# Another order of the 52 tiles of the first input projection

## The chip, the cores and the metric

The kernel runs on one core of a Trainium2 chip. The metric is the device time of one execution in microseconds; of the kernel before there are three runs, with a median of 2320.35 us (2316.67 to 2329.12). A profile of one more execution shows what each engine did: TensorE (PE, with its weight loads as PEld), VectorE (DVE), ScalarE (ACT), GpSimd (POOL) and SyncE (SP), which issues the DMAs.

## The reference

One inference step of a two-layer decoder for a prompt of 512 tokens and 8 x 4 sample tokens (544 columns in all), float32, width 2048. The first ("even") layer:

```python
h = x @ w_in                       # 2048 -> 6784 = 53 blocks of 128
h_sh, gate_a, q_b, k_b, v_b, gate_b, q_m, gate_m = _split(h, (...))
prev = concatenate([shift0[:, None], h_sh[:, :-1]])
y_a, s_new = rwkv7_mix(h_sh + (prev - h_sh) * mu, ...)   # 12 heads x 64, a recurrence
y_b = combine(...)                 # dilated windows: 3 groups x 4 heads x 64
y_m = memory_attention(q_m, mkv)   # 4 heads x 128, 256 memory tokens
u = concatenate([y_a * silu(gate_a), y_b * silu(gate_b), y_m * silu(gate_m)])
x = layer_norm(ALPHA * x + u @ w_out, ln_g, ln_b)
```

The second ("odd") layer has the same frame with a retention branch. Both groups of tokens share all weights; the sample tokens also read cached keys, values and states. Returned are the two outputs and all new states.

## The kernel before

Everything is laid out with features in partitions and the 544 tokens in columns. A *tile* is one block of 128 output features of a projection. Its 16 blocks of weights are loaded by SP (two halves, four buffers in all), split into a high part by ACT and a low part by DVE, and multiplied with the split activations in three matmuls per block (`three`, line 469), for two halves of 272 columns: 96 matmuls a tile. Behind each half, ACT (for gates also DVE) evacuates it (`done`).

The tiles run in one list (`Main.run`, line 481): eight tiles for the memory keys and values, then the 53 tiles of the first input projection, the output projection, and the second layer. The first projection begins with the tile of the two small `lora` inputs (`r18`, place 0 here); the other 52 follow in the order of the string `ORDER0` (line 2206), each letter taking the next tile of its kind. I call the letters places 1 to 52. The kinds:

- `r`: the 18 blocks of the shifted input of the recurrence, in six triples; with the third of a triple the *pair* of heads is complete and its work is started (pairs 0 to 5; `hsh_done`, line 793). An `r` tile asks for two work buffers and keeps one.
- `q` and `m`: the four queries of the memory attention, and its four gates.
- `b`: the 18 blocks of the dilated windows, for two head pairs: three queries, three keys, three values each. The ninth starts the first head pair's softmax (`b_prompt`), the twelfth the sample keys (`b_keys`), the eighteenth the second softmax and the sample values.
- `a` and `c`: the six gates of the recurrence (one for each pair) and the two of the windows.

All else that a layer does is *side work*: generators (`spawn`, line 302) that a planner at build time steps in between the matmuls of the tiles, two matmul triples apart (`pump`, line 327), by priority. It runs on a model of the engines' clocks; what comes out is a fixed order of instructions for each engine. A pair's work is a long chain: `rwkv_pre` (preparation, priority 1, begins with a load of `lora` weights), `rwkv_solve` (a triangular solve in 31 steps on DVE, instructions of 102 partitions), `rwkv_chain` (eight chunks of small dependent matmuls), `rwkv_sample` (loads `rwkv_s`, started when half of the chain is done) and `rwkv_norm`, which stores the result to `yad`; a gate tile reads it back, multiplies, and the product is split for the output projection.

Side work and tiles share 41 work buffers of 128 x 576 floats (tag `P`). A pair reserves 13 of them before its `lora` load (`open`, line 107), a softmax 8, the sample keys 7, the sample values 9. A reservation begins only when that many are free beyond what is promised to others. A tile that needs a buffer where all free ones are promised makes the planner step side work alone until one comes free (`drive`, line 339):

```python
def page(self, dt=F32, cols=PAGE, own=None, wait=True):
    if wait and own is None and self.avail('P') <= self.held():
        self.drive(lambda: self.avail('P') > self.held())
```

The output projection takes its 12 blocks of gated results in the order in which their gates stand in `ORDER0` (`out_order`, line 2211), and its first tile drives side work until the blocks are there (`Gated.mov`, line 1877).

Of the kernel before, what the change touches and what calls it, by code (L numbers as in the profile page):

```python
# [2202 lines left out]


MEM0 = (0, 1, 2, 3, 4, 5, 6, 7)
ORDER0 = 'rrqrbbqrqqrrrrrmbrmbbbrbrmbrbmarrbabrarraabbbbbbbcca'
ORDER1 = '0000000011111111222222223333333344444444qqqq55555555mmmm'
SPILL1 = (0, 1, 2, 3, 4, 5, 6, 7, 8, 9)

# [1 line left out]
def out_order():  # L2211

    ks0, ks = [], {'a': list(range(6)), 'c': [6, 7], 'm': list(range(8, 12))}
    for ch in ORDER0:
        if ch in ks:
            ks0.append(ks[ch].pop(0))
    ks1, left = [], {c: ORDER1.count(c) for c in ORDER1}
    for ch in ORDER1:
        left[ch] -= 1
        if ch == 'm':  # L2220
            ks1.append(15 - left[ch])
        elif ch != 'q' and left[ch] < 2:
            ks1.append(2 * int(ch) + 1 - left[ch])
    return ks0, ks1


def body(nc, tc, A, npages=41, stop=None):
    from contextlib import ExitStack
    with ExitStack() as es:
# [92 lines left out]
        ks0, ks1 = out_order()  # L2322
        for ch in ORDER0:
            order.append(kinds[ch].pop(0))
# [256 lines left out]
```

## Time and profile before

| | us |
|---|---|
| median of three runs | 2320.35 |
| the profiled execution | 2316.73 |
| its span, first to last instruction | 2314.9 |
| TensorE busy | 2206.6 (95%) |
| VectorE, ScalarE, GpSimd busy | 1294.8, 980.8, 296.1 |
| mean granted clock of TensorE | 0.977 |

Of TensorE's time, the matmuls of the tiles take most; the first input projection lies between about 58 and 1034 us. Busy times are unions over an engine's instructions. A granted clock of 1.00 is 2.4 GHz, and 0.5 is the lower level of 1.2 GHz; a mean between them says what part of a stretch was at which level.

### The profile page before, as it was taken

What the parts mean: (1) busy time and instruction counts of PE and PEld (TensorE: products, weight loads), DVE (VectorE), ACT (ScalarE), POOL (GpSimd) and SP (SyncE); (2) the same over time, 40 slices, a digit from 0 to 9 for tenths busy, and PEclk for the clock granted to TensorE, in tenths of its full rate; (3) what the DMA queues carried; (4) which work ended last, traced back from release to release, by engine and by line L of the source; (5) the groups of instructions that cost most, each with busy time, mean ns of one, the idle gap of its engine ahead of it and who ended that gap; (6) DMA issues with size and microseconds to landing.
All of it is one profiled execution on the core that took longest, in us unless ns stands there. A gap on an engine that the chain in (4) does not pass through costs nothing. (4 is left out here: it accounts for less than half of the span.)

```text
span 2314.9 us, 46280 instructions
## 1 busy us (share of the span) xinstructions
PE 2206.6 (95%) x18633; PEld 2118.7 (92%) x18633; DVE 1294.8 (56%) x2718; ACT 980.8 (42%) x2286; POOL 296.1 (13%) x445
## 2 busy tenths in 40 slices
PE   8999999889998999998989999999999999999996
PEld 8999898778998989887979999999999999999996
DVE  6367468637656766355788444444444433347686
ACT  6344453356244444343577323232323243235464
POOL 0000000000000000002665000000000000003474
PEclk9999999989999999998999999999999999999998
DMA  9222532312221424528757443424343424445662
GB/s 328 99 72 78 202 99 85 103 52 98 76 71 52 122 82 130 189 72 275 211 164 249 161 131 102 134 99 137 97 137 97 141 84 171 144 167 183 214 205 100
DMA packets 149714, 313.46 MB, mean 135 GB/s; under 512 B 39376, under 2 KB 48536, under 8 KB 149500
## 3 DMA queue, kind: packets, MB, share of 16 engines
q1 hardware_dynamic: 149500, 310.51, 41.3%
q8 instruction: 146, 2.39, 0.4%
q14 instruction: 68, 0.56, 0.1%
HBM read 271.38 MB, written 39.07 MB: 134 GB/s over the span
## 5 line engine op out<-in xcount | busy, mean ns | idle before, releaser
L194 PE MATMUL m<-xh,wh 128*128 128x272 f32 (+1 forms) x4448 | 1323.5, 298 | 9.4 <-ACT wh L227 3.8
L194 PE MATMUL m<-xh,wl 128*128 128x272 f32 (+1 forms) x4448 | 1289.3, 290 | 8.7 <-DVE wl L235 8.6
L194 PE MATMUL m<-xl,wh 128*128 128x272 f32 (+1 forms) x4448 | 1286.1, 289 | 3.5 <-DVE xl L235 3.5
L194 PEld LDWEIGHTS m<-xh,wh 128*128 128x128 f32 x4448 | 845.0, 190 | 23.6 <-issue 9.5
L194 PEld LDWEIGHTS m<-xh,wl 128*128 128x128 f32 x4448 | 842.6, 189 | 11.8 <-DVE wl L235 11.7
L194 PEld LDWEIGHTS m<-xl,wh 128*128 128x128 f32 x4448 | 845.1, 190 | 6.8 <-DVE xl L235 3.8
L235 DVE TENSOR_TENSOR wl<-wr,wh 128x512 fp32r<-128x512 f32 (+1 forms) x752 | 548.1, 760 | 445.5 <-ACT wh L227 439.6
L227 ACT ACTIVATE wh<-wr 128x512 fp32r<-128x512 f32 (+1 forms) x752 | 419.1, 604 | 248.2 <-PE m L194 230.1
L235 POOL TENSOR_TENSOR P<-P,P 128x272 f32<-128x272 f32 (+1 forms) x242 | 244.7, 1033 | 897.6 <-ACT P L227 733.5
L194 PE MATMUL s<-P,P 128*128 128x128 f32 (+11 forms) x3808 | 331.9, 283 | 27.7 <-ACT P L227 15.6
L194 PEld LDWEIGHTS s<-P,P 128*128 128x128 f32 (+6 forms) x3808 | 256.4, 145 | 73.1 <-ACT P L227 22.0
L227 ACT ACTIVATE P<-m 128x272 f32<-128x272 f32 (+3 forms) x253 | 93.8, 379 | 513.4 <-PE m L194 513.0
L235 DVE TENSOR_TENSOR P<-P,P 128x544 f32<-128x544 f32 (+24 forms) x576 | 279.7, 497 | 54.5 <-ACT P L227 34.8
L227 ACT ACTIVATE P<-s 64x64 f32<-64x64 f32 (+9 forms) x581 | 160.1, 291 | 346.9 <-PE s L194 121.6
L227 ACT ACTIVATE P<-P 64x64 f32<-64x64 f32 (+5 forms) x284 | 124.6, 451 | 125.4 <-POOL P L235 72.7
L240 DVE SCALAR_TENSOR_TENSOR P<-P,m 128x272 f32<-128x272 f32 x116 | 50.4, 435 | 134.2 <-ACT P L227 97.8
L284 POOL MEMSET P<- 128x576 f32 (+6 forms) x104 | 28.9, 291 | 569.3 <-PE s L194 316.0
L194 PE MATMUL m<-P,wh 128*128 128x256 f32 x352 | 68.5, 295 | 8.3 <-ACT wh L227 6.4
L209 PE MATMUL s<-cst,P 128*128 128x128 f32 (+2 forms) x409 | 64.5, 283 | 12.1 <-ACT P L227 8.8
L194 PEld LDWEIGHTS m<-P,wh 128*128 128x128 f32 x352 | 57.7, 201 | 9.3 <-ACT wh L227 6.6
L267 DVE TENSOR_REDUCE P<-P 102x1 f32<-102x2 f32 (+16 forms) x193 | 60.9, 315 | 6.7
L209 PEld LDWEIGHTS s<-cst,P 128*128 128x128 f32 (+2 forms) x409 | 49.3, 142 | 15.0 <-ACT P L227 9.1
(69 smaller groups left out, 926.9 us busy)
## 6 DMA issues: line engine op xcount, KB each, us to landing
wr<-w_in SPq DMA_DIRECT2D x218, 512.0 KB
wr<-w_out SPq DMA_DIRECT2D x64, 512.0 KB
wr<-w_out SPq DMA_DIRECT2D x64, 384.0 KB
wr<-w_mem SPq DMA_DIRECT2D x26, 512.0 KB
P<-ret_s SPq DMA_DIRECT2D x48, 256.0 KB
o_ret_s<-P SPq DMA_DIRECT2D x48, 256.0 KB
P<-dk SPq DMA_DIRECT2D x36, 256.0 KB
P<-dv SPq DMA_DIRECT2D x36, 256.0 KB
```

The source lines that it names most:

```text
L194: self.nc.tensor.matmul(out, lhsT, rhs, start=start, stop=stop, skip_group_check=True)
L209: self.nc.tensor.transpose(out, in_, ident)
L227: self.nc.scalar.activation(out, in_, func, **kw)
L235: e.tensor_tensor(out, a, b, op=op)
L240: self.nc.vector.scalar_tensor_tensor(out, a, s, b, op0=op0, op1=op1)
L267: self.nc.vector.tensor_reduce(out, a, axis=AX.X, op=op)
L284: e.memset(out, v)
```

## The change

One string: the order of the 52 tiles. The tiles themselves, the side work and its priorities and all sizes stay. The order of the blocks in the output projection follows from the string: before it is the four `m`, five `a`, two `c`, the last `a`; after it is the four `m`, four `a`, the first `c`, two `a`, the second `c`.

```diff
 MEM0 = (0, 1, 2, 3, 4, 5, 6, 7)
-ORDER0 = 'rrqrbbqrqqrrrrrmbrmbbbrbrmbrbmarrbabrarraabbbbbbbcca'
+ORDER0 = 'rrrbbqrqqqrrrrrrmbmbbbrbbmbrrrbrmaabrarrbacabbbbbbac'
 ORDER1 = '0000000011111111222222223333333344444444qqqq55555555mmmm'
```

## Rows read from the trace of the kernel before

**Rows 1.** The page: span, and busy us (share of the span) and instructions by engine.

```profile
span 2314.9 us, 46280 instructions
...
PE 2206.6 (95%) x18633; PEld 2118.7 (92%) x18633; DVE 1294.8 (56%) x2718; ACT 980.8 (42%) x2286; POOL 296.1 (13%) x445
...
PEclk9999999989999999998999999999999999999998
```

**Rows 2.** Busy us of engines by stage: PE, PEld, DVE, ACT, POOL, granted clock, DMA share, GB/s.

```profile
106.80:311.30 204.50, 201.64 (x1699) 190.06 (x1698) 114.14 (x292) 95.26 (x255) 11.09 (x44) 0.99 0.35 115
311.30:445.50 134.20, 125.60 (x1045) 121.40 (x1044) 103.64 (x283) 53.35 (x119) 5.34 (x30) 0.99 0.33 98
445.50:594.80 149.30, 126.38 (x944) 116.95 (x946) 89.24 (x208) 74.06 (x209) 4.24 (x21) 0.89 0.23 72
775.50:937.10 161.60, 150.13 (x1366) 143.00 (x1369) 102.55 (x258) 71.94 (x195) 6.98 (x26) 0.97 0.38 119
1034.00:1068.60 34.60, 24.17 (x454) 19.96 (x453) 12.48 (x45) 12.85 (x26) 1.26 (x4) 0.70 0.91 323
1260.00:2100.00 840.00, 840.00 (x6823) 819.82 (x6823) 353.43 (x688) 280.63 (x614) 14.77 (x18) 1.00 0.39 132
```

**Rows 3.** Waits of PE, 70 to 1069 us: total us, times, longest.

```profile
PE s L194 <- ACT P L227: 15.6, 15, 2.1
PE s L209 <- ACT P L227: 8.8, 1, 8.8
```

**Rows 4.** Busy us by stage again, for the stretch around place 25.

```profile
445.50:480.00 34.50, 21.03 (x169) 18.58 (x167) 17.74 (x42) 11.42 (x39) 1.11 (x5) 0.65 0.22 56
```

**Rows 5.** Timeline of ACT: evacuations of tiles; start us, us, instruction, idle before.

```profile
106.80 0.40 ACT L227 ACTIVATE P<-m 128x272 f32<-128x272 f32 x1 [1.97 <-PE m L194]
...
123.17 0.37 ACT L227 ACTIVATE P<-m 128x240 f32<-128x240 f32 x1 [1.67 <-PE m L194]
...
445.50 0.40 ACT L227 ACTIVATE P<-m 128x272 f32<-128x272 f32 x1 [1.97 <-PE m L194]
...
474.60 0.40 ACT L227 ACTIVATE P<-m 128x272 f32<-128x272 f32 x1
...
554.59 0.37 ACT L227 ACTIVATE P<-m 128x240 f32<-128x240 f32 x1 [0.63 <-PE m L194]
...
775.52 0.38 ACT L227 ACTIVATE P<-m 128x240 f32<-128x240 f32 x1 [1.98 <-PE m L194]
```

**Rows 6.** Timeline of SP: DMA issues of the pairs, the keys and the softmax.

```profile
120.67 0.42 SPq L288 DMA_DIRECT2D P<-lora  x1
...
293.27 0.38 SPq L288 DMA_DIRECT2D P<-lora  x1
...
316.40 0.33 SPq L288 DMA_DIRECT2D yad<-P  x1
316.82 0.38 SPq L288 DMA_DIRECT2D P<-lora  x1
...
471.01 0.42 SPq L288 DMA_DIRECT2D P<-rwkv_s  x1
...
517.48 0.38 SPq L288 DMA_DIRECT2D P<-lora  x1
...
798.01 0.42 SPq L288 DMA_DIRECT2D yad<-P  x1
798.47 0.43 SPq L288 DMA_DIRECT2D P<-lora  x1
...
914.15 0.43 SPq L288 DMA_DIRECT2D P<-dk  x1
...
959.78 0.38 SPq L288 DMA_DIRECT2D P<-c_bmask  x1
...
1054.46 0.33 SPq L288 DMA_DIRECT2D yad<-P  x1
```

**Rows 7.** Timeline of DVE: the end of pair 2's solve, and what follows.

```profile
459.98 0.52 DVE L267 TENSOR_REDUCE P<-P 102x11 f32<-102x352 f32 x1
460.53 0.28 DVE L240 SCALAR_TENSOR_TENSOR P<-s,P,P 64x64 f32<-64x64 f32 x1
```

**Rows 8.** Timeline of PE: the first matmul of the output projection that waits.

```profile
1062.84 0.60 PE L194 MATMUL m<-xl,wh 128*128 128x272 f32 x1 [3.46 <-DVE xl L235]
```

## The prediction

> **What bounds the kernel now.** I read the profile from the outside in. First the line of busy times and the line of TensorE's clock by slices [rows 1]: TensorE is busy for 95% of the span, so every stall on it counts, and no other engine comes near. Then the busy times by stage [rows 2], to see where the missing 5% sits. From 1260 to 2100 us, in the second layer, TensorE is busy for 840.00 of 840.00 us at a granted clock of 1.00: nothing can be won there. The change lies in the first input projection and what follows on it, and there the stages leave idle 2.9 us of 204.5, 8.6 us of 134.2, 22.9 us of 149.3, 11.5 us of 161.6 and, in the 34.6 us before the first tile of the output projection, 10.4 us. The order of the tiles can move these losses, the clock lost beside them, and nothing else.
>
> Next the waits of TensorE over the projection [rows 3]: no wait is long in sum, the largest being 15.6 us in 15 pieces, but one single piece has 8.8 us. Its stage by itself [rows 4] shows the dearest place of the kernel: from 445.5 to 480.0 us TensorE is busy for 21.0 of 34.5 us at a clock of 0.65. The evacuations [rows 5] say which tile that is: the tile at place 24 ends at 445.50, and the first half of place 25 is evacuated only at 474.60, 29.1 us on, where half a tile takes 5.9 us when nothing stands in between (840.00 us for 6823 matmuls [rows 2] is 0.123 us each, 48 a half). Counted along the code, one work buffer is free there and one is promised, and an `r` tile asks for two, so the program is written with side work in between until pair 1 gives up its reservation: its sample part starts at 471.01 [rows 6]. The DVE row says why that was slow [rows 7]: pair 2's triangular solve holds VectorE until 460.50 and pair 1's next update runs right behind it.
>
> The SP rows [rows 6] show that the same 41 buffers string the pairs together. Each pair loads its `lora` weights once it has got its 13 buffers. Pair 2's load (316.82) stands right behind pair 0's last store (316.40), pair 3's at 517.48 behind pairs 1 and 2 giving up theirs, pair 5's (798.47) right behind pair 3's last store (798.01). Pair 5's last store is at 1054.46, and the output projection's first tile waits for its gated result until 1062.84 [rows 8]. So the projection's end is set by a chain of buffers: pair 3, pair 5, place 52's gate.
>
> **The change part by part.** No instruction is added or removed: each tile keeps its 96 matmuls, its weight loads and splits. Beside the 52 tiles, the order in which the output projection takes its blocks changes with the string, at no cost in instructions. After places 15, 24 and 40 the same tiles have been done in both orders; the changes are moves between these points.
>
> (1) Pair 0 is complete at place 3 instead of 4. Before, place 3 is a `q` and its end is at 106.80, pair 0's last tile ends at 123.17 [rows 5], and its load is at 120.67 [rows 6]. After, the load comes at about 106.8 minus the same lead, so 14 to 16 us sooner. Pair 1 got its buffers at 293.27, when pair 0's chain was through; I move that by the same 14 us. Pair 2 gains less: its last tile stays at place 15. The edit itself costs nothing; its cover is side work, since mem attention's first head moves three places back.
>
> (2) Place 25 is a `b`, which asks for one buffer, instead of an `r`, which asks for two. The free buffer is promised, so it still has to wait for pair 1. But pair 1 should be 14 us further: its release at about 457 instead of 471. The price of the stall now: 34.5 - 21.0 = 13.5 us idle; the clock 0.65 means 24.2 us at the lower level (1.2 GHz), of which 24.2 - 13.5 = 10.7 us were busy at half speed, losing 5.3 us; together 18.8 us. The buffer was wanted at about 451 (445.50 + 5.9) and the release came at 471, 20 us later; 14 us sooner, 6 of these 20 remain, and with what pair 1 loses again by (3), 8. I take 11 us saved (18.8 x 12/20), with 0 (pair 1 no sooner) and 18.8 (no stall at all) as bounds.
>
> The Trainium skill, TensorE: Matmul & The Clock Gate, "Terms", prices a throttled stretch at its time multiplied by the missing share of the clock. By that the 24.2 us would cost 12.1 us beside the idle 13.5, so 25.6 us, and 12/20 of it would be 15 us instead of 11. The rows have most of the low stretch idle, and idle time loses nothing twice, so the sum above stays with 18.8.
>
> (3) Place 16 is an `r` (two buffers) instead of an `m` (one). By the count, five buffers are free there and four promised, so the second request waits, until pair 1 gives up its key buffer. That is a new stall, of the kind of place 25 but in another state: pair 1 and pair 2 both have preparation work to run, and no solve stands on VectorE. Queued behind it are this tile's evacuation and all later tiles. Its bounds are 0 (place 15 asked for a buffer in the same way, and its stage from 106.8 to 311.3 has only 2.9 us idle in all [rows 2]) and 12 us (two thirds of the stall of place 25). I take 4 us, nearer to the row next to it.
>
> (4) Pair 3 is complete at place 28 instead of 25, behind two more `b` and an `m`. Place 28 ends at 554.59 now [rows 5]; 7 us sooner by (2) and (3), so 548. Pair 3's buffers came at 517.48, so it starts 30 us later. Pair 4 is complete one place sooner (32 for 33), and the first head pair's softmax, which hands back sixteen buffers, starts two places sooner. Pair 5 is complete at place 40 in both (775.52). It must wait for pair 3's last release (now 798.01). How much of the 30 us arrives there is not to be read from the trace: pair 3 takes 280.5 us from load to store (517.48 to 798.01), pair 5 256.0, pair 0 195.7, so a pair that starts in a calmer stretch can win back 24 us and more. Bounds for the start of pair 5: 0 and 30 us late from this alone.
>
> (5) The last `b` query (and with it the sample keys) goes from place 43 to 41, one `c` from 50 to 43, the last `b` from 49 to 50, and the `c` of the second head pair becomes the last tile in place of pair 5's gate. The keys ran from 914.15 until the next load behind them at 959.78, 45.6 us [rows 6]; they were waiting for seven buffers. Earlier keys fill TensorE earlier, and the second softmax (959.78, released by the keys' end) can start as soon as its tile is done. On SP the keys' 36 loads move ahead of later weight loads, which are hidden by four weight buffers in flight. The tail's price today: 10.4 us idle, and at a clock of 0.70 20.8 us at the lower level, 10.4 of them busy, so 5.2 more: 15.6 us. For (4) and (5) together the bounds are 15.6 us saved and 45.6 us lost (the keys wholly ahead of pair 5). I take 3 us lost: the later pair 3 mostly made good, the rest from a pair 5 that ends slightly later.
>
> The sum: -11 + 4 + 3 = -4 us. The profiled execution took 2316.73 us, its span being 2314.9 and 1.8 us lying around it; so 2312.7 us for such an execution. The median shown is 2320.35, 3.6 us above the profiled one, and half of that added gives 2314.5. I predict 2314 us.
>
> **The rivals.** A change of 0.5%, 11.6 us, is about what a measurement of this kernel can tell from none.
>
> Rival A, faster: the stall of place 25 goes whole (-18.8), place 16 asks while side work covers it (0), and the keys, done early, leave a tail with half its loss (-7.8). 2316.7 - 26.6 = 2290, with the median's offset about 2294. For it: the loads of pairs 1 and 2 and the release at 471.01 hang on buffers that come sooner. Against it: at equal points the same tiles hold the same buffers, so a wait avoided tends to reappear at the next request.
>
> Rival B, slower: the sample keys, now asked for at the end of place 41, take seven buffers while pair 5 still looks for thirteen. Place 41 ends at 775.52 + 11.8 - 7 = 780 at the earliest, pair 3's last release is at 798 or later, so the order turns round wherever that release falls behind the end of place 41. Then pair 5 waits for the keys' 45.6 us, of which the calm stretch behind the last tile gives back about 20 (half of the 60 us between pair 5's 256.0 and pair 0's 195.7, less 10 for the lower clock there): +25.6. With the stall of place 25 as forecast: -11 + 4 + 25.6 = +18.6, so about 2337 to 2340. Against it: pair 5 is served first when both could be.
>
> Rival C, the change does not do what it says: place 25 waits as long as before, with a `b` in the place of the `r`, because pair 1's release hangs on VectorE's queue and not on pair 0. Then 2316 to 2323.
>
> **How the numbers follow.** Forecast (2306 to 2324) 0.34, A (2288 to 2306) 0.30, B (2330 to 2350) 0.24, C 0.12. Of the forecast 0.06 lies more than 0.5% below 2320.35, of B 0.02 within 0.5%. So faster 0.30 + 0.06 = 0.36, same 0.28 + 0.12 + 0.02 = 0.42, slower 0.22. The range leaves out the lowest 0.08 and the highest 0.10: 2292 to 2342; the forecast's own is 2306 to 2324. The sums of the bounds (-34.4 and +57.6) lie beyond both.
>
> **What would show it.** Step 1 is right if the first `lora` load falls near 106 and the third pair's load moves little. Step 2: the first half of place 25 within 20 us of place 24's end, and a clock above 0.65 there. Step 3: a low-clock stretch near 315. Step 4: the fourth load near 548. Step 5 and rival B: whether the first `dk` load stands ahead of the sixth `lora` load, and when the sixth pair's last store comes against 1054.46. The prediction is wrong if the output projection's first tile starts earlier than 1045 or later than 1080, or if a new stall of over 10 us shows between places 26 and 40.

## The result, and the profile after

The changed kernel takes 2287.6 us (median of 4 runs, 2282.8 to 2290.0) against 2318.5 us before (the median of the three runs and the profiled execution): a ratio of 0.9855, 95% interval 0.982 to 0.9889. It is faster by 1.4%, more than the prediction's range allowed (2292 to 2342); rival A had named 2288 to 2306. The medians differ by 30.9 us. The profiled execution took 2290.0 us, the slowest of the four, with a span of 2288.2, which is 26.7 us below the span of before.

The page of the changed kernel: span, busy us by engine, TensorE's clock by slices.

```profile
span 2288.2 us, 46280 instructions
...
PE 2201.4 (96%) x18633; PEld 2114.9 (92%) x18633; DVE 1294.2 (57%) x2718; ACT 979.0 (43%) x2286; POOL 290.3 (13%) x445
...
PEclk9999999999999999999999999999999999999998
```

The instructions are the same in number, as on [rows 1]. After places 15, 24 and 40, and again when the first half of the output projection's first tile is evacuated, the same tiles lie behind both kernels, so the span can be cut there and compared piece by piece. The ends of these places are 311.3, 445.5, 775.5 and 1068.6 us before and 310.5, 446.6, 756.5 and 1033.3 after. That gives -0.8 us up to place 15, +1.9 from there to 24, -20.1 from 24 to 40, -16.3 from 40 to the output projection, and +8.6 from there to the end: together -26.7.

Busy times by stage, first of before over the last three pieces, then of after (columns as in [rows 2]: PE, PEld, DVE, ACT, POOL, clock, DMA share, GB/s).

```profile
445.50:775.50 330.00, 298.54 (x2362) 279.16 (x2361) 205.96 (x511) 152.12 (x411) 13.64 (x54) 0.94 0.25 76
775.50:1068.60 293.10, 270.57 (x2904) 246.37 (x2904) 157.45 (x410) 120.99 (x330) 10.73 (x36) 0.94 0.42 137
1068.60:2314.90 1246.30, 1210.58 (x9856) 1182.92 (x9854) 661.81 (x1136) 504.78 (x1061) 252.91 (x258) 0.99 0.46 151
```

```profile
446.60:756.50 309.90, 293.31 (x2365) 274.29 (x2364) 203.25 (x503) 146.45 (x401) 11.38 (x54) 0.97 0.26 80
756.50:1033.30 276.80, 262.13 (x2648) 240.45 (x2647) 150.29 (x381) 124.15 (x333) 9.98 (x36) 0.96 0.40 131
1033.30:2288.20 1254.90, 1219.39 (x10108) 1189.74 (x10106) 663.63 (x1153) 504.67 (x1061) 250.67 (x258) 0.99 0.47 153
```

Between places 24 and 40 TensorE does the same work (2362 and 2365 matmuls) with 16.6 us idle instead of 31.5, at a better clock. That is a true gain. The 16.3 us of the next piece are partly a move: 256 matmuls of side work fewer are done there (2904 to 2648), and 252 more behind it. Half of what was gained, 8.6 us, comes back in the output projection and later; 7.7 us stay.

The stretch around place 25, as [rows 4], then waits of TensorE over the projection, as [rows 3] (of after, its two longest sums).

```profile
446.60:481.10 34.50, 30.50 (x281) 27.73 (x280) 17.87 (x45) 20.18 (x69) 1.10 (x6) 1.00 0.32 92
```

```profile
PE s L194 <- ACT P L227: 23.6, 24, 3.7
PE d L194 <- DVE P L235: 5.7, 9, 2.7
```

In 34.5 us there are now 30.5 us of work at full clock, where there were 21.0 at 0.65. The one wait of 8.8 us is gone, and no wait is longer than 3.7.

ACT's evacuations of tiles, to be read against [rows 5]: place 3's end, place 24's end, the first half of place 25, place 28's end, the end of place 52.

```profile
106.24 0.46 ACT L227 ACTIVATE P<-m 128x240 f32<-128x240 f32 x2 [1.97 <-PE m L194]
...
446.64 0.40 ACT L227 ACTIVATE P<-m 128x272 f32<-128x272 f32 x1 [1.97 <-PE m L194]
...
459.81 0.40 ACT L227 ACTIVATE P<-m 128x272 f32<-128x272 f32 x1
...
550.43 0.46 ACT L227 ACTIVATE P<-m 128x240 f32<-128x240 f32 x2 [7.33 <-PE m L194]
...
1023.97 0.40 ACT L227 ACTIVATE P<-m 128x272 f32<-128x272 f32 x1
```

SP's issues for the pairs, the softmaxes and the first of the sample keys, against [rows 6].

```profile
105.48 0.42 SPq L288 DMA_DIRECT2D P<-lora  x1
...
275.65 0.54 SPq L288 DMA_DIRECT2D P<-lora  x1
...
320.51 0.42 SPq L288 DMA_DIRECT2D P<-lora  x1
...
515.42 0.42 SPq L288 DMA_DIRECT2D P<-c_bmask  x1
...
553.73 0.54 SPq L288 DMA_DIRECT2D P<-lora  x1
...
625.26 0.38 SPq L288 DMA_DIRECT2D P<-lora  x1
...
762.36 0.36 SPq L288 DMA_DIRECT2D o_rwkv_s<-P  x1
762.81 0.39 SPq L288 DMA_DIRECT2D P<-lora  x1
...
830.64 0.35 SPq L288 DMA_DIRECT2D yad<-P  x1
...
883.42 0.91 SPq L288 DMA_DIRECT2D P<-dk  x2
...
969.24 0.32 SPq L288 DMA_DIRECT2D yad<-P  x1
969.65 0.38 SPq L288 DMA_DIRECT2D P<-c_bmask  x1
```

SP before, the first softmax and pair 4, which [rows 6] leave out:

```profile
572.93 0.44 SPq L288 DMA_DIRECT2D P<-c_bmask  x1
...
671.58 0.38 SPq L288 DMA_DIRECT2D P<-lora  x1
```

DVE after, the end of pair 2's solve, against [rows 7], and the stage between the end of place 52 and the output projection:

```profile
451.85 0.52 DVE L267 TENSOR_REDUCE P<-P 102x11 f32<-102x352 f32 x1
```

```profile
1024.00:1033.30 9.30, 9.30 (x131) 9.21 (x128) 6.02 (x17) 7.01 (x18) 0.00 (x0) 1.00 0.92 322
```

Pair 1's load is 17.6 us sooner, pair 2's solve ends 8.1 us sooner, and pair 5 tells the most. It starts at 762.81, 35.7 us sooner and 67.8 us *ahead* of pair 3's last store (830.64), behind which it stood before. Its own last store comes at 969.24 instead of 1054.46, long before the last tile ends at 1023.97. The output projection then waits for nothing (TensorE is busy for 9.30 of the 9.30 us).

### The profile page after: what moved, and what is told of

It is laid out like the page before. It is cut to its first block, busy times and chain, and to the rows that moved or that the text cites. A ratio compares the mean times of both kernels' runs of the same rounds, so it can differ in the third digit from the quotient of the medians.

```text
span 2288.2 us, 46280 instructions
## 1 busy us (share of the span) xinstructions
PE 2201.4 (96%) x18633; PEld 2114.9 (92%) x18633; DVE 1294.2 (57%) x2718; ACT 979.0 (43%) x2286; POOL 290.3 (13%) x445
## 5 line engine op out<-in xcount | busy, mean ns | idle before, releaser
L194 PEld LDWEIGHTS m<-xh,wh 128*128 128x128 f32 x4448 | 847.1, 190 | 17.7 <-issue 11.4
L194 PEld LDWEIGHTS m<-xl,wh 128*128 128x128 f32 x4448 | 847.4, 191 | 2.7 <-issue 1.4
L194 PE MATMUL s<-P,P 128*128 128x128 f32 (+11 forms) x3808 | 324.0, 277 | 25.3 <-ACT P L227 19.7
L194 PEld LDWEIGHTS s<-P,P 128*128 128x128 f32 (+6 forms) x3808 | 250.7, 142 | 68.4 <-ACT P L227 28.3
L235 DVE TENSOR_TENSOR P<-P,P 128x544 f32<-128x544 f32 (+25 forms) x576 | 280.0, 497 | 44.3 <-ACT P L227 29.4
L240 DVE SCALAR_TENSOR_TENSOR P<-P,s 128x512 f32<-128x512 f32 x66 | 44.0, 684 | 33.5 <-PE s L194 32.1
```

The lines of the kernel that those rows point to most:

```text
L194: self.nc.tensor.matmul(out, lhsT, rhs, start=start, stop=stop, skip_group_check=True)
L235: e.tensor_tensor(out, a, b, op=op)
L240: self.nc.vector.scalar_tensor_tensor(out, a, s, b, op0=op0, op1=op1)
```

## The experiments

All ratios are to the kernel before, timed on the same chip. The order of before has 'rrqrbbqrqqrrrrr' at places 1 to 15, 'mbrmbbbrb' at 16 to 24, 'rmbrbmarrbabrarr' at 25 to 40 and 'aabbbbbbbcca' at 41 to 52; each diff shows the places that are edited. The expectations number their theories as they came: theory 6 of e7 and e8 (the sample keys) is not theory 6 of e9 (pair 1's buffers).

**One part of the change at a time.** The first four runs take the new order over one stretch and leave the rest old.

```diff
 e1, places 1 to 15
-rrqrbbqrqqrrrrr
+rrrbbqrqqqrrrrr
```

> The new order for places 1 to 15 alone (pair 0 complete at place 3), the old one behind. Theory 1 (two stretches with two causes: the stall at place 25 goes because pair 0 is complete sooner, the wait before the output projection goes because the first softmax and so pairs 4 and 5 get their buffers sooner): about 2299 us, 19 less than before, place 25's first half within 15 us of place 24's end, but still 10 us or more idle before the output projection. Theory 2 (all follows from pair 0 being sooner): about 2288 us, both stretches gone. Theory 3 (the wait before the output projection goes by the new order of the last twelve places): 2299 us, as theory 1.

Measured: 2292.4 us, ratio 0.9889 (0.9865 to 0.9913). By the ratios about three quarters of the gain come from this stretch alone, though the two intervals overlap. From place 24's end to 26's, with the same tiles as before, it takes 50.8 us (441.9 to 492.7) instead of 69.0: 18.3 us less, where the prediction had priced the whole stall at 18.8.

```diff
 e2, places 25 to 40
-rmbrbmarrbabrarr
+bmbrrrbrmaabrarr
```

> The new order for places 25 to 40 alone. Theory 1: place 25 waits as long as before (its first half about 29 us behind place 24's end), the first softmax load near 540 instead of 573, the fifth lora load near 650 or sooner, no wait before the output projection: about 2301 us, 17 less. Theory 2: about 2318 us, nothing gone. Theory 3: about 2318 us.

Measured: 2296.1 us, 0.99 (0.9885 to 0.9915). Place 25, a `b` here, still comes 28.9 us behind place 24 (442.3 to 471.2): the single buffer of the `b` is not what removes the stall. The gain lies further on. The first softmax is loaded at 530.7 instead of 572.9, pair 5's load comes at 769.8, its result at 1027.2, and the output projection starts at 1050.6.

```diff
 e3, places 41 to 52
-aabbbbbbbcca
+bacabbbbbbac
```

> The new order for places 41 to 52 alone. Theory 1: both stretches stay, about 2318 us; slower by up to 15 us if pair 5, still late, now also waits for buffers that the keys took. Theory 2: about 2318 us. Theory 3: the wait before the output projection goes, about 2301 us.

Measured: 2320.9 us, 0.9997 (0.9981 to 1.0014), nothing.

```diff
 e4, places 1 to 40
-rrqrbbqrqqrrrrrmbrmbbbrbrmbrbmarrbabrarr
+rrrbbqrqqqrrrrrrmbmbbbrbbmbrrrbrmaabrarr
```

> The new order for places 1 to 40, the old one for the last twelve. Theory 1: as the changed kernel, about 2288 us (2283 to 2295). Theory 2: the same. Theory 3: about 2299 us, with the wait before the output projection still there.

Measured: 2303.6 us, 0.993 (0.9912 to 0.9947), slower by the median than places 1 to 15 alone (the intervals just touch). So the parts don't add. e1 and e2 each take away the wait before the output projection (between place 52's end and there TensorE is busy for 9.0 of 9.4 us in e1 and 9.0 of 9.2 in e2), and that can be won only once. They do it by two routes: in e1 pair 5's load (770.7) stands right behind pair 3's last store (769.4), which is early; in e2 it comes 55 us ahead of that store (769.8 and 824.7). The last twelve places are worth nothing on the old order, and some 16 us behind the new 1 to 40. None of the three theories fits all four runs: theory 1 left a wait before the output projection in e1, theory 2 gave e2 nothing, theory 3 gave e3 17 us, and theories 1 and 2 miss e4 by 16 us.

**What in the first fifteen places does it.** Two edits of two places each.

```diff
 e5, places 3 and 4 (pair 0 complete one place sooner)
-rrqrbbqrqqrrrrr
+rrrqbbqrqqrrrrr
 e6, places 7 and 8 (second query behind the fourth r; pair 0 as before)
-rrqrbbqrqqrrrrr
+rrqrbbrqqqrrrrr
```

> One swap alone: places 3 and 4, so that pair 0 is complete at place 3; all else as before. Theory 1 (place 25's stall goes because pair 0 is complete sooner): the stall is gone, about 2299 us (2290 to 2305), first lora load near 106. Theory 4 (it goes because the second and third query stand behind the fourth r tile, so that memory attention's work comes later beside pair 0's solve): the first lora load near 106 too, but place 25's first half still 25 us or more behind place 24's end, about 2318 us.

Measured: 2317.8 us, 0.999 (0.9973 to 1.0007). Pair 0's load comes at 104.5, its result 21 us sooner than before (295.3 for 316.4), and yet pair 1's load stays at 293.7 and place 25 stalls. The prediction's ground for step 2, pair 0 drawing pair 1 along, is refuted.

> Places 7 to 10 alone in the new order (r, then three queries, for query, r, two queries); pair 0 stays complete at place 4. Theory 1: the stall of place 25 stays, about 2318 us. Theory 4: the stall is gone with pair 0 no sooner (first lora load near 120), about 2298 us.

Measured: 2306.4 us, 0.9923 (0.99 to 0.9947). Pair 0 is no sooner (121.0), pair 1's load comes at 280.2, and place 25 follows 10.0 us behind 24 (451.5 to 461.6). One swap of a query with an `r` takes the stall away. Not all of it is won, since place 24 itself takes longer: from place 23's end to 25's it is 42.6 us for 54.5 before.

**Is it pair 1's buffers?** e9 is e1 with one condition more: pair 1 may not ask for its buffers before place 14.

```diff
 e9, on e1
 def rwkv_pre(g, p):
+    while p == 1 and len(g.hs) < 9:
+        yield em.clk['pe'] + 500
     own = t.own = yield from em.open(13)
```

> The order is that of the first experiment (the new places 1 to 15, the old ones from 16 on), where the stall at place 25 cost 1.4 us and pair 1's load came at 277.1. One thing is added: pair 1 may not ask for its 13 buffers until place 14 has been written, when it got them in the kernel before. The tiles, the work and pair 0's times stay. Theory 6 (the stall at place 25 goes because pair 1 gets its buffers before the memory attention's sample part has spread, whatever the order): second lora load at 288 to 297, first half of place 25 evacuated 22 to 32 us behind place 24's end, 14 to 19 us lost there, and the run 12 to 20 us longer than the first experiment, 2304 to 2322 us. Rival (the order of the queries does it, by the later memory attention, and pair 1's time is only a companion): place 25 within 16 us as in the first experiment, time 2288 to 2299 us.

Measured: 2321.1 us, ratio 1.0004 (0.9988 to 1.002). SP around pair 1's load, e1 and then e9:

```profile
277.08 0.54 SPq L288 DMA_DIRECT2D P<-lora  x1
...
278.19 0.86 SPq L288 DMA_DIRECT2D P<-memv  x2
```

```profile
288.22 0.33 SPq L288 DMA_DIRECT2D P<-memv  x1
...
292.02 0.33 SPq L288 DMA_DIRECT2D yad<-P  x1
292.44 0.38 SPq L288 DMA_DIRECT2D P<-lora  x1
```

And the evacuations of place 24's end and place 25's first half, e1 and then e9:

```profile
441.88 0.40 ACT L227 ACTIVATE P<-m 128x272 f32<-128x272 f32 x1 [1.97 <-PE m L194]
455.01 0.40 ACT L227 ACTIVATE P<-m 128x272 f32<-128x272 f32 x1
```

```profile
445.54 0.40 ACT L227 ACTIVATE P<-m 128x272 f32<-128x272 f32 x1 [1.97 <-PE m L194]
474.76 0.40 ACT L227 ACTIVATE P<-m 128x272 f32<-128x272 f32 x1
```

With the order the same and pair 1 15.4 us later, the stall is back (29.2 us between the halves, 13.1 in e1). So is the whole of e1's gain lost, since pairs 3 to 5 slip too: pair 5's load goes from 770.7 to 798.4, its result from 983.1 to 1058.0. The rows show who is in front: in e1 pair 1 gets its buffers ahead of the first values of the memory attention (`memv`), in e9, as before, only behind the last. By the code the sample part reads up to eight blocks ahead, the last four of them only where buffers are to spare (`ahead`, line 99), so it and pair 1 ask for the same free buffers. Pair 1 need not be ahead of the values, though: in e6 all sixteen are issued in one go from 256.6 to 268.7, before pair 1's load at 280.2, and are out of its way. Over both kernels and all twelve experiments the place 25 stall is there when pair 1's load comes at 290 or later (before, e2, e3, e5, e9: 28.9 to 29.4 us from place 24's end to place 25's first half), and gone when it comes by 281 (9.3 to 13.2 us in the other nine). e9 sets pair 1's time by hand, but it does not move pair 1 alone: pair 2's load comes 12.0 us sooner than in e1 (309.8 for 321.8). Pair 2's time by itself is not what counts, since it is 311.3 in e6, without the stall. But the lead of pair 1's load over pair 2's parts the fourteen kernels as cleanly as pair 1's time: 16.6 to 23.6 us in the five with the stall, 31.1 to 47.0 in the nine without. No run here parts these two readings.

**Why pair 5 is early.** e10 is the changed kernel with the first softmax held for two places.

```diff
 e10, on the changed kernel
 def b_prompt(g, hp):
+    while hp == 0 and len(g.hs) < 14:
+        yield em.clk['pe'] + 500
     own = yield from em.open(8)
```

> The changed kernel with one thing added: the first softmax may not ask for its eight buffers until place 29 has been written (it asked for them behind place 27). Theory 7 (the last pairs come early in the changed kernel because the first softmax hands back its buffers early): first softmax's load at 535 to 560 instead of 515.4, pair 4's load 20 to 60 us later than 625.3, pair 5's 20 to 80 us later than 762.8, possibly behind the sample keys, which is the order that rival B of the prediction speaks of; then the output projection starts 10 to 60 us later and the run takes 2298 to 2350 us. Rival (pair 5 comes early because pairs 1 and 2 come through early): pair 5's load at 755 to 775 as before, output projection at 1030 to 1042, time 2284 to 2296 us.

Measured: 2304.6 us, 0.9933 (0.9912 to 0.9954). SP, the first softmax, pair 4, the first keys, pair 3's and pair 5's marks:

```profile
551.10 0.38 SPq L288 DMA_DIRECT2D P<-c_bmask  x1
...
633.55 0.62 SPq L288 DMA_DIRECT2D P<-lora  x1
...
783.46 0.94 SPq L288 DMA_DIRECT2D P<-dk  x2
...
803.73 0.33 SPq L288 DMA_DIRECT2D yad<-P  x1
...
825.00 1.58 SPq L288 DMA_DIRECT2D P<-dk  x3
...
833.93 0.38 SPq L288 DMA_DIRECT2D P<-lora  x1
...
1045.45 0.33 SPq L288 DMA_DIRECT2D yad<-P  x1
```

The softmax is 35.7 us late, pair 4 only 8.3 (20 to 60 were expected), but pair 5 71.1 us: the keys get their seven buffers first and pair 5's thirteen come after them. This is rival B, made by hand. The wait stands before the output projection, from 969.6 (place 52's end) to 1063.0:

```profile
969.60:1063.00 93.40, 76.58 (x967) 60.63 (x967) 40.26 (x115) 34.33 (x100) 1.44 (x5) 0.71 0.41 136
```

Its price, 17.0 us by the medians (2304.6 against 2287.6), is of the order of the +25.6 that the prediction set for it, and below it. Its condition was what didn't come about. The hold also lets pair 3 start 21.3 us sooner (532.4 for 553.7), and pair 5 is late all the same. e2 agrees from the other side: there the softmax is early (530.7) and pair 1 late (290.1), and pair 5's load is early (769.8).

**What the last twelve places do.** Three orders with the new places 1 to 40.

```diff
 e7 (first c at 43), e8 (last query b at 41), e11 (first c at 44)
-aabbbbbbbcca
+aacbbbbbbbca
+baabbbbbbcca
+aabcbbbbbbca
```

> The new order for places 1 to 40 and, in the old order of the last twelve, one gate of the windows moved from place 50 to 43. Theory 5 (the last twelve places gain because the first c tile asks for its buffer early, where one is to be had, instead of at place 50, where the sample keys and the second softmax hold them): about 2288 us or less, the losses from place 40 to the output projection 25 us or less instead of the 36 of places 1 to 40 alone. Theory 6 (they gain because the twelfth b tile and with it the sample keys come sooner): as places 1 to 40 alone, about 2303 us.

Measured: 2290.7 us, 0.9857 (0.9837 to 0.9877), as fast as the change.

> The new order for places 1 to 40 and, in the old order of the last twelve, the twelfth b tile moved from place 43 to 41. Theory 5: about 2303 us, as places 1 to 40 alone. Theory 6: about 2288 us.

Measured: 2300.2 us, 0.9904 (0.9887 to 0.992). No more than e4, within the intervals. But the keys are only asked for sooner, not served sooner: their first load is at 829.5, at 829.8 in e4. So theory 6 is not tested by this run; what speaks against it is e7, where the keys come later (847.4) and the kernel is faster.

> The new places 1 to 40, then the old last twelve with the first c at place 44 (it was at 43 in the seventh experiment, which took 2290.7 us, and at 50 in the kernel before). Theory 5 (what decides in the last twelve is that no c asks for a buffer while the keys and the last softmax hold them): any place up to 45 will do, output projection at 1030 to 1045, 2284 to 2294 us. Rival (43 just hits a gap): a stall of 5 to 15 us at place 44, 2296 to 2306 us.

Measured: 2302.0 us, 0.9926 (0.991 to 0.9942). One place later and the gain of e7 is gone; from place 40 to the output projection TensorE is idle for 27.5 us, for 14.7 in e7. SP behind pair 3's last store in e11, and TensorE's wait at place 44:

```profile
829.53 0.34 SPq L288 DMA_DIRECT2D yad<-P  x1
829.92 0.43 SPq L288 DMA_DIRECT2D P<-c_dmask  x1
830.72 4.08 SPq L288 DMA_DIRECT2D P<-dk  x4
```

```profile
829.96 0.38 PE L194 MATMUL s<-P,P 128*128 128x128 f32 x2
838.97 0.42 PE L194 MATMUL s<-P 128*128 128x32 f32 x1 [8.63 <-ACT P L227]
```

The same keys at 829.5 to 830.7 and a wait of 8.5 to 8.6 us stand in e4 and e8; in e7 and the changed kernel the keys come at 847.4 and 883.4 and there is no such wait. Counted along the code, the buffers that pair 3 hands back make seven free, just enough for the keys, and then none is left for the next tile. A `c` at place 43 has taken one of them, the keys must wait for more, and the tiles go on. Theory 5 was right that a `c` decides and wrong in what it needs: it must hold its buffer before pair 3 ends, not merely stay clear of the keys.

**A version to beat both.**

```diff
 e12, all places
-rrqrbbqrqqrrrrrmbrmbbbrbrmbrbmarrbabrarraabbbbbbbcca
+rrrbbqrqrqqrrrrmmbbrbbrbrmbrbmarrbbarrraaabbbabbbbcca
```

> An order put together from what the experiments show: pair 0 complete at place 3, the fourth query behind the fifth r, no place that asks for two buffers while pairs 1 and 2 hold theirs (place 25 is an r, but two of the b come before it at places 18 and 19), the ninth b at place 29, the second c next to last. If the theories 4 to 7 hold: second lora load at or before 280, no half tile between places 16 and 40 that comes more than 12 us behind the one before, output projection at 1025 to 1040, 2278 to 2290 us. If the changed kernel's order has something that they don't name: 2292 to 2310 us.

Measured: 2292.5 us, 0.9875 (0.9854 to 0.9895), not faster than the change, and with overlapping intervals not told apart from it. Pair 1's load comes at 273.4, and place 25 has no loss at all (TensorE is busy for all of the 9.3 us between the halves). But place 26's first half comes 19.3 us behind place 25, at a clock of 0.82, where 12 us was the mark. From place 40 to the output projection it takes 290.8 us against 276.8, so that the latter starts at 1047.6 and not by 1040. That is mostly moved work: 443 matmuls more are done there (3091 to 2648) at about the same idle time (14.4 and 14.7 us), and behind it e12 takes 1243.1 us for 1254.9. The time stands at the lower edge of the range for something unnamed, and its runs (2283.7 to 2295.4) lie in both ranges, so it doesn't settle whether the theories name all that the change holds.

## Why the prediction was wrong

Rival A named the outcome and the prediction didn't believe in its size; what let pairs 1 and 5 come early is in neither. By its own mark, an output projection that starts before 1045, it was wrong: 1033.3. By its own steps:

**Step 1** held in its numbers (first load at 105.5, third at 320.5) and failed in its reason. Pair 1 came 17.6 us sooner, more than the 14 predicted, but not because pair 0 did (e5): with the second query behind the fourth `r`, pair 1 and the memory attention's values no longer stand in each other's way (e6), and held back by hand it brings the stall back (e9). The prediction had taken "pair 1 got its buffers when pair 0's chain was through" from two neighbouring rows and never looked at who else was asking.

**Step 2** is the first term that was mis-sized. It left 8 of 20 us of the wait and took 11 us saved; the first half of place 25 came at 13.2 us behind place 24, under the 20 it had set as its own mark, at a clock of 1.00, and the stall went all but whole (4.0 of the 34.5 us are still idle). With the same tiles (e1) that is 18.3 us. It had carried pair 1's 14 us one to one to the release. But the release also hung on VectorE [rows 7], where two chains meet: pair 2's solve ends 8.1 us sooner, and pair 1, whose own solve is through 19.5 us sooner (SP loads its results, `td`, at 395.18 for 414.64), has less left to do behind it. That this lead is the reason is my reading; no run holds it alone. SP, pair 1's `td`, before and then after:

```profile
414.64 2.74 SPq L288 DMA_DIRECT2D P<-td  x6
```

```profile
395.18 3.85 SPq L288 DMA_DIRECT2D P<-td  x6
```

The loss by the prediction's account, 18.8 us, was about the right price; the Trainium skill's rule ("Terms" of TensorE: Matmul & The Clock Gate) gave 25.6, which 18.3 does not bear out. The stages from place 24's end to 26's say the same, before and then e1:

```profile
445.50:514.50 69.00, 50.94 (x382) 46.28 (x381) 34.18 (x84) 29.92 (x109) 2.33 (x10) 0.80 0.18 51
```

```profile
441.90:492.70 50.80, 43.95 (x375) 39.54 (x374) 27.22 (x65) 28.46 (x103) 2.42 (x10) 1.00 0.24 68
```

Idle time plus half of the busy low time is 22.8 us before and 6.9 in e1, 16.0 apart; idle time plus the time multiplied by the missing share is 31.9 and 6.9, 25.0 apart. Both are estimates from these rows; the 18.3 us lie nearer the first.

**Step 3** did not happen. Place 16's first half comes 4.6 us behind place 15 (310.5 to 315.1), at full clock. The count of buffers had pair 2's promise standing already at place 16; pair 2 gets its buffers only at 320.5. +4 is 0.

**Step 4** is the step that failed. Its first half came true: pair 3 starts 36.3 us later (553.73 for 517.48) and ends 32.6 us later. "Pair 5 must wait for pair 3's last release" did not. The wait was read from two rows that stand together [rows 6], 798.01 and 798.47, as if the one store were the only source of buffers. The first softmax, 57.5 us sooner (515.42 for 572.93), hands back its buffers sooner, pair 4 starts 46.3 us sooner (625.26 for 671.58), and pair 5 has its thirteen buffers 6.3 us behind its last tile (762.81, place 40's end being at 756.5). It still stands right behind pair 3, but behind the store of its state (`o_rwkv_s`, 762.36), 68 us ahead of its last release. The prediction names this early softmax and gives it no number. e10 shows its worth: hold it back and pair 5 is 71.1 us later.

**Step 5**: the keys were 30.7 us sooner, as forecast in direction, and behind pair 5, against rival B. What counts is the `c` at place 43, which keeps the keys off the last buffers when pair 3 ends (e7 against e11: 11.4 us by the medians). The prediction had listed that move without a price. For steps 4 and 5 it took +3; the tail of 15.6 us went whole, while 8.6 us of moved work came back behind it, so -7.7.

Sum: predicted -11 + 4 + 3 = -4; measured, by the cuts above, +1.1 up to place 24, -20.1 from 24 to 40, -7.7 behind it. The argument held against rival A, that an avoided wait tends to reappear at the next request, did not hold for the change as a whole, though e4 (place 44) and e12 (place 26) show waits that come up again: as I read the runs, the waits were not one shortage passed on, but two chains that met at a bad moment. Once the earlier chain was ahead, it stayed ahead, in e1 down to pair 5. The rivals were priced as if the terms were independent, while e1 and e9 show that one of them, pair 1's load, pulls both.

Rival A's sum was -26.6, and the spans differ by -26.7; that they agree to the tenth is in part luck. Its first two terms came true: the stall went all but whole, and place 16 cost nothing. Its third, a tail with half its loss (-7.8) because the keys are done early, came out at -7.7 for another reason: the wait went whole because pair 5 was early, and half of that gain was work moved behind it. (Rival A's 2294 also adds the whole 3.6 us to the median, where the forecast adds half; by the forecast's measure it is 2292.)

What stays open: why the changed kernel does more side work behind the first projection than e7 at the same total time; whether it is pair 1's time or its lead over pair 2 that counts at place 25; and whether an order that holds all that the experiments name can beat the change, since e12 neither did nor kept all its marks.

## What to carry to other kernels

Where work units reserve buffers from one pool, an order acts through who asks first. List for each request on the critical chain everybody else who asks in that stretch, readers that run ahead included; don't take the release that stands beside it in the trace for the only one. Compare kernels at points where the same work is done, and check whether a gain in one stage is work moved to the next. And test a suspected early start by holding just that one start back: one condition (e9) turned 1.1% of gain into none.
